# Odd token tiles on the other half of TensorE's columns, and late gate chunks beside the attention

## The chip, the cores and the metric

One Trainium2 chip, one core of it. The metric is the device time of one execution in microseconds (us), lower is better. A kernel is timed several times and the median is quoted; one more execution is taken with the hardware profiler, and every row below is from that one.

## The reference, cut to what matters

A decoder layer over 16 meta tokens and 2048 tokens of width 1024. One wide projection feeds three causal mixers with 4 heads of 128 each, a sigmoid gate weighs each mixer's projection, and the gated sum goes through `w_out`.

```
q, k, v  -> stick_breaking_attention            # o_sb, all earlier keys, blocks of 128
gq,gk,gv -> conv of width 4, silu, l2norm -> gated_delta_rule_chunked   # o_gd, unit lower triangular solves
hq,hf,hi -> hgrn2_chunked                       # o_hg, decayed scores within a chunk, a state between chunks
y   = gates[0]*(o_sb @ w_branch[0]) + gates[1]*(o_gd @ w_branch[1]) + gates[2]*(o_hg @ w_branch[2])
out = h + y @ w_out
```

## The kernel before, in words

The 2048 tokens are four **quarters** j = 0 to 3 of 512 tokens, each four **token tiles** of 128 (`NT = 4`, index n). The residual width lies on the 128 partitions in 8 pieces. Numbers are float32; a product of two such values is made of three matmuls of 128x512 (`mm3`, lines 167 to 169: high by high, high by low, low by high).

**Dense work** is the generator `dense_work`. Its unit is a **chunk**: 24 matmuls of 128x512 that project the 512 tokens on 128 columns of `w_in` (`proj`), followed by one evacuation. In a quarter there are 16 chunks for the attention (`sb_proj`: K, Q, V, gate for 4 heads), one small one (`gdn_rows`), 12 **conv chunks** for the delta rule (`gdn_proj`, `conv`), 4 gates, 16 for HGRN2, 24 **mix gate chunks** (`branch`, 8 for each mixer, evacuated by one sigmoid on ScalarE, line 1212) with 24 **products** of 12 matmuls each, and 8 output chunks (`outp`). A conv chunk gives VectorE three multiply-adds (line 730) and one product (line 734).

**Scans** are the parts with a chain of dependent steps. `sb_scan` is one head's attention: scores `z` on TensorE, two sigmoids on ScalarE (lines 522, 523), a running product on VectorE (line 528), a multiply (line 534, VectorE and GpSimd by turns), then four transposes (line 558), a copy to the high part (line 562, ScalarE), the low part (line 118, VectorE), and three matmuls into `av`. In quarter j it runs over j+1 blocks of keys. `gdn_mats` and `gdn_scan` are the delta rule: `gdn_scan` inverts 32x32 blocks on VectorE, joins them to 64x64 (lines 920 to 944) and to 128x128 (its **last step**, lines 959 and 969), then runs the recurrence over the token tiles (lines 991 to 1014). `hg_scan` is HGRN2 for one head: seven **levels** s = 1, 2, 4, ..., 64, with a matmul per token tile and block in each. Levels 1 to 16 (line 1148) use all four quarters of the output partitions, level 32 (line 1135) two of them (b and b+32 rows from b = 0 and 64), level 64 (line 1126) the lower half alone; ScalarE copies what 32 and 64 give into `at` (lines 1140 and 1130).

**The order.** The main loop weaves each scan with a counted number of dense chunks: a chunk ends with an `END`, `adv(n)` emits n of them, `weave(scan, us, n)` spreads n over a scan by the estimated times in the list `US`. In quarter j, `adv(5)` and four attention scans (4, 4, 4 and 5 chunks) come first, then `gdn_mats` (3 each), `gdn_scan` (11), and so on. The program is then built with `schedule_with_timeline_sim=True`: a scheduler reorders what was emitted, within the buffers, so that a stretch of the built program can hold more dense chunks than its `weave` counted. Each engine runs its own list in that order. A product of mixer 0 needs the attention of all four heads (`obs[0, h]`), and the gate tiles of mixers 0 and 1 have two buffers (`g`), so before the last head is done at most two or three mix gate chunks can run.

Of the kernel before, what the change touches and what calls it, by code (L numbers as in the profile page):

```python
# [39 lines left out]
def kernel(  # L40
# [830 lines left out]
    def gdn_scan(j, st):  # L871
# [82 lines left out]
        for g in range(2):  # L954
            pT = (p_z, p_tr)[g]()
            pT3 = pT.rearrange("p (h n c) -> p h n c", h=2, n=NT)
            for h in range(2):
                for n in range(NT):
                    nc.tensor.matmul(
                        pT3[64:128, h, n], u[2 * g + h][0:64, n, 64:128], x2[g][0:64, h, n], start=True, stop=True  # L960
                    )
            (nc.scalar.copy, nc.vector.tensor_copy)[g](x2[g][64:128], pT3[64:128])
        yield 2.0
        for g in range(2):
            pU = (p_z, p_tr)[g]()
            pU3 = pU.rearrange("p (h n c) -> p h n c", h=2, n=NT)
            for h in range(2):
                for n in range(NT):
                    nc.tensor.matmul(
                        pU3[0:64, h, n], x2[g][64:128, h, n], u[2 * g + h][64:128, n, 64:128], start=True, stop=True  # L970
                    )
                (nc.scalar.copy, nc.vector.tensor_copy)[g](u[2 * g + h][0:64, :, 64:128], pU3[0:64, h])
# [121 lines left out]
    def hg_scan(j, h, st):  # L1094
# [10 lines left out]
        while s < P:  # L1105
# [17 lines left out]
            if s == 64:  # L1123
                for n in range(NT):
                    c = META + n * P
                    nc.tensor.matmul(
                        z[:64, n * 64 : (n + 1) * 64], kql[:, c : c + 64], kql[:, c + 64 : c + P],
                        start=True, stop=True,
                    )
                nc.scalar.copy(at[:64, :, 64:], z[:64, :256].rearrange("p (n c) -> p n c", n=NT))  # L1130
            elif s == 32:
                for n in range(NT):
                    for b in (0, 64):
                        c = META + n * P + b
                        nc.tensor.matmul(
                            z[b : b + 32, n * 32 : (n + 1) * 32], kql[:, c : c + 32], kql[:, c + 32 : c + 64],
                            start=True, stop=True,
                        )
                for b in (0, 64):
                    nc.scalar.copy(  # L1140
                        at[b : b + 32, :, b + 32 : b + 64],
                        z[b : b + 32, :128].rearrange("p (n c) -> p n c", n=NT),
                    )
# [60 lines left out]
    def branch(j, xs, b, obs, y, yh, yl, lag=0):  # L1204

        gs, ws = {}, {}

        def gate(e):
            gs[e] = slot("D", (P, TQ)) if b == 2 else slot("g", (P, TQ))
# [5 lines left out]
        def product(e):  # L1215
# [8 lines left out]
            if b == 0:  # L1224
                y[e] = slot("y", (P, TQ))
# [77 lines left out]

    def dense_work():
# [39 lines left out]
    US = (  # L1344
        [CHUNK_US] * 29 + [B_US] * 5 + [CHUNK_US] * 4 + [B_US] * 3 + [CHUNK_US] * 8 + [B_US] * 2
        + [CHUNK_US] * 4 + [B_US] * 2 + [CHUNK_US] * 4 + [B_US] * 4 + [CHUNK_US] * 4 + [B_US] * 4
        + [3 * END] * 4 + [CHUNK_US] * 8
    )

# [15 lines left out]
    def weave(scan, scan_us, n):  # L1365

        upto = ends[0] + n
        us = sum((US + US)[ends[0] % len(US) :][:n])
# [76 lines left out]
    for j in range(nq):  # L1445
        adv(5 if j else 3)
        sb_us = 4 * (2.0 + 2.7 * j) + 0.8 * (5 + 4 * j)
        for h in range(H):
            obs[0, h] = weave(sb_scan(j, h, sst), sb_us, 4 + (h == H - 1))
        for h in range(H):  # L1450
# [4 lines left out]
        adv(5)  # L1455
        for h, o_ in enumerate(weave(both(hg_scan(j, 0, hst), hg_scan(j, 1, hst)), 2 * HG_US, 7)):
            obs[2, h] = o_
        adv(5)
# [90 lines left out]
```

## Time and profile before

| | |
|---|---|
| median of 3 runs | 2812.92 us (2812.78 to 2814.28) |
| the profiled execution, its own time | 2815.66 us |
| its span, first to last instruction | 2813.9 us |
| TensorE busy / VectorE / ScalarE / GpSimd | 98% / 52% / 34% / 26% of the span |
| mean granted TensorE clock | 0.995 of full speed |

The span is what the trace shows; 1.8 us of the profiled execution's time lie outside it. Busy time of TensorE counts overlapping matmuls once. A 128x512 matmul is shown as some 0.39 us long, but the next starts 0.23 us after it, so its cost is read from start to start. A float32 matmul that is not split by hand (lines 920 to 1185) stands in the trace as two instructions.

### The profile page before, as it was taken

The page shows a single profiled execution, that of the slowest core. Times are in us where ns is not written, and L with a number is a line of the kernel's source. Part 1 is how long each engine was busy: PE and PEld are TensorE (multiplying, and loading weights), DVE is VectorE, ACT ScalarE, POOL GpSimd, SP SyncE. Part 2 cuts the span into 40 slices and gives each one's busy share as a digit, 9 for nine tenths or more (in the row PEclk, how much of TensorE's full clock was granted, in tenths as well). Part 3 has the DMA queues.
Part 4 walks back from the last instruction along what each step waited for, and adds up shares of the span by engine and source line. Part 5 has one row for each costly group of instructions (what it writes and reads, how often), then busy time and mean ns, then how long its engine had stood idle before and what let it go on. Part 6 is the DMA issues. An engine that isn't in the chain of part 4 may idle for free.

```text
span 2813.9 us, 46012 instructions
## 1 busy us (share of the span) xinstructions
PE 2758.2 (98%) x17616; PEld 2273.7 (81%) x17616; DVE 1469.7 (52%) x2878; ACT 953.8 (34%) x2195; POOL 738.4 (26%) x1011
## 2 busy tenths in 40 slices
PE   7999999999999999999999999999999999999999
PEld 7898787888887888878887778887888777788887
DVE  5466637745357545543256754454325677527521
ACT  5454234243345212222244531221224555113120
POOL 4555214433132302112023330111212222302111
PEclk9999999999999999999999999999999999999999
DMA  7667746679554654547754356344764434653556
GB/s 256 228 202 250 256 163 218 227 256 322 188 172 149 193 170 130 152 149 249 228 177 161 129 164 187 121 150 151 246 211 145 135 119 143 196 160 125 158 157 210
DMA packets 200064, 520.51 MB, mean 185 GB/s; under 512 B 43104, under 2 KB 44064, under 8 KB 199844
## 3 DMA queue, kind: packets, MB, share of 16 engines
q1 hardware_dynamic: 199556, 517.50, 56.6%
q8 instruction: 139, 2.28, 0.3%
q14 instruction: 81, 0.66, 0.1%
q10 hardware_dynamic: 288, 0.07, 0.0%
HBM read 397.18 MB, written 120.31 MB: 184 GB/s over the span
## 4 chain that ended last, share of the span: by engine, by line
PE 90%; DVE 5%; DMA 2%; ACT 1%; issue 1%; POOL 1%; SPq 0%; DVEq 0%; POOLq 0%; ACTq 0%
PE acc L167 21%; PE acc L168 20%; PE acc L169 20%; PE av L167 4%; PE av L168 4%; PE av L169 4%; PE tr L558 2%; PE acc L380 1%; PE tr L380 1%; DVE D L730 1%; PE z L167 1%; PE z L168 1%; PE z L169 1%; PE z L1148 1%; PE z L832 1%
## 5 line engine op out<-in xcount | busy, mean ns | idle before, releaser
L167 PE MATMUL acc<-xh,w 128*128 128x512 f32 (+2 forms) x2224 | 854.2, 384 | 5.7 <-DMA w<-wk 1.8
L168 PE MATMUL acc<-xl,w 128*128 128x512 f32 (+2 forms) x2224 | 839.6, 378 | 0.3 <-DVE xl L260 0.2
L169 PE MATMUL acc<-xh,w 128*128 128x512 f32 (+2 forms) x2224 | 837.4, 377 | 1.3 <-DVE w L118 1.3
L167 PEld LDWEIGHTS acc<-xh,w 128*128 128x128 f32 x2224 | 422.5, 190 | 82.0 <-DMA w<-wk 2.6
L169 PEld LDWEIGHTS acc<-xh,w 128*128 128x128 f32 x2224 | 422.6, 190 | 74.7 <-DVE w L118 2.0
L168 PEld LDWEIGHTS acc<-xl,w 128*128 128x128 f32 x2224 | 422.3, 190 | 68.7 <-DVE xl L260 1.3
L528 DVE TENSOR_TENSOR_SCAN S<-S,zero 128x128 f32<-128x128 f32 (+4 forms) x216 | 195.9, 911 | 129.6 <-ACT S L522 114.5
L118 POOL TENSOR_TENSOR w<-wraw,w 128x512 fp32r<-128x512 f32 x106 | 148.8, 1405 | 292.1 <-ACT w L147 269.9
L534 POOL TENSOR_TENSOR S<-S,S 128x256 f32<-128x256 f32 (+2 forms) x108 | 93.8, 869 | 355.2 <-DVE S L528 234.1
L522 ACT ACTIVATE S<-z,rq 128x128 f32<-128x128 f32 (+4 forms) x216 | 117.0, 542 | 125.7 <-PE z L169 80.7
L147 ACT CAST w<-wraw 128x512 fp32r<-128x512 f32 x182 | 112.5, 619 | 134.5 <-PE acc L169 63.3
L730 DVE SCALAR_TENSOR_TENSOR D<-D,cw,D 128x512 f32<-128x512 f32 (+1 forms) x144 | 124.6, 866 | 18.2 <-ACT D L728 16.2
L167 PE MATMUL av<-xh,w 128*128 128x512 f32 (+2 forms) x328 | 128.8, 393 | 1.1 <-ACT D L1050 1.1
L167 PE MATMUL acc<-ob,w 128*128 128x512 f32 x316 | 127.1, 404 | 2.1 <-ACT ob L401 1.4
L168 PE MATMUL av<-xl,w 128*128 128x512 f32 (+2 forms) x328 | 127.6, 389 | 0.0
L169 PE MATMUL av<-xh,w 128*128 128x512 f32 (+2 forms) x328 | 127.1, 388 | 0.0
L118 DVE TENSOR_TENSOR S<-tr,S 128x512 fp32r<-128x512 f32 (+4 forms) x176 | 104.9, 605 | 41.6 <-ACT S L562 41.2
L168 PE MATMUL acc<-ob,w 128*128 128x512 f32 x316 | 126.4, 401 | 0.0
L169 PE MATMUL acc<-ob,w 128*128 128x512 f32 x316 | 124.9, 396 | 0.0
L523 ACT ACTIVATE S<-z,rq 128x128 f32<-128x128 f32 (+4 forms) x216 | 116.4, 539 | 1.0 <-POOL S L527 0.9
L562 ACT CAST S<-tr 128x512 fp32r<-128x512 f32 (+4 forms) x176 | 91.2, 530 | 63.5 <-PE tr L558 63.4
L1230 POOL TENSOR_TENSOR y<-y,g 128x512 f32<-128x512 f32 x32 | 45.2, 1416 | 256.7 <-DVE g L1228 256.7
(386 smaller groups left out, 4931.1 us busy)
## 6 DMA issues: line engine op xcount, KB each, us to landing
w<-wk SPq DMA_DIRECT2D x555, 512.0 KB, 3.5
wk<-w SPq DMA_DIRECT2D x184, 512.0 KB, 3.6
wraw<-in_w_in_dram SPq DMA_DIRECT2D x142, 256.0 KB, 3.8
D<-in_xq_dram SPq DMA_DIRECT2D x56, 256.0 KB, 4.3
S<-rows SPq DMA_DIRECT2D x48, 256.0 KB, 4.9
S<-dv SPq DMA_DIRECT2D x48, 256.0 KB, 4.3
out_dram<-D SPq DMA_DIRECT2D x32, 256.0 KB, 4.3
S<-dk SPq DMA_DIRECT2D x24, 264.0 KB, 4.5
```

The lines of the kernel that those rows point to most:

```text
L118: (eng or nc.gpsimd).tensor_sub(out_, a, hi.bitcast(F32))
L147: nc.scalar.copy(hi, raw)
L167: nc.tensor.matmul(dst, lh, rh, start=first, stop=False)
L168: nc.tensor.matmul(dst, lh, rl, start=False, stop=False)
L169: nc.tensor.matmul(dst, ll, rh, start=False, stop=last)
L380: nc.tensor.transpose(pt[:, n * P : (n + 1) * P], src[:, META + n * P : META + (n + 1) * P], ident)
L522: nc.scalar.activation(pc[:, :n], z[:, :n], AF.Sigmoid, scale=rq[:, NT + i : NT + i + 1])
L523: nc.scalar.activation(at[:, :n], z[:, :n], AF.Sigmoid, scale=rq[:, i : i + 1])
L528: nc.vector.tensor_tensor_scan(pc[:, 0:n][:, ::-1], pc[:, 0:n][:, ::-1], zero1.broadcast_to([P, n]), 1.0 if carry[i] is None else pc[:, n ...
L534: eng.tensor_mul(at[:, :n], at[:, :n], pc[:, 1 : n + 1])
L562: nc.scalar.copy(ath[:kw, cs_], tr[:kw, cs_])
L730: nc.vector.scalar_tensor_tensor(dst[:, c0:], raw[:, c0 + i : c0 + i + n], cw[:, ci, i : i + 1], dst[:, c0:], ALU.mult, ALU.add)
```

## The change

First, three groups of small matmuls send odd token tiles to another part of the output partitions. Level 64: tiles 1 and 3 write partitions 64 to 127 instead of 0 to 63. Level 32: tiles 1 and 3 write 32 rows further up, so that all four quarters are used. Last step of the inverses: tiles alternate between the halves. Each copy that follows becomes two, one for the even tiles and one for the odd tiles.

Second, in quarters 2 and 3 (`j >= AHEAD`) the branch of mixer 0 runs with a lag of 5: its first five gate chunks are emitted directly behind `sb_proj`, three gates with products follow behind `gdn_proj`, and the last five products behind the first head's HGRN2 chunks. These gates lie in the tiles `y`, of which there are eight, and the product is written over the gate. The counts of the main loop and the list `US` follow. Quarters 0 and 1 are emitted as before.

```diff
         for g in range(2):
             pT = (p_z, p_tr)[g]()
-            pT3 = pT.rearrange("p (h n c) -> p h n c", h=2, n=NT)
+            pT3 = pT[:, :256].rearrange("p (h n c) -> p h n c", h=2, n=2)
             for h in range(2):
                 for n in range(NT):
+                    o = 64 * (1 - n % 2)
                     nc.tensor.matmul(
-                        pT3[64:128, h, n], u[2 * g + h][0:64, n, 64:128], x2[g][0:64, h, n], start=True, stop=True
+                        pT3[o : o + 64, h, n // 2], u[2 * g + h][0:64, n, 64:128], x2[g][0:64, h, n],
+                        start=True, stop=True,
                     )
-            (nc.scalar.copy, nc.vector.tensor_copy)[g](x2[g][64:128], pT3[64:128])
+            for i in range(2):
+                o = 64 * (1 - i)
+                (nc.scalar.copy, nc.vector.tensor_copy)[g](x2[g][64:128, :, i::2], pT3[o : o + 64])
...
                 for n in range(NT):
+                    o = 64 * (n % 2)
                     nc.tensor.matmul(
-                        pU3[0:64, h, n], x2[g][64:128, h, n], u[2 * g + h][64:128, n, 64:128], start=True, stop=True
+                        pU3[o : o + 64, h, n // 2], x2[g][64:128, h, n], u[2 * g + h][64:128, n, 64:128],
+                        start=True, stop=True,
                     )
...
                 for n in range(NT):
-                    c = META + n * P
+                    c, o = META + n * P, 64 * (n % 2)
                     nc.tensor.matmul(
-                        z[:64, n * 64 : (n + 1) * 64], kql[:, c : c + 64], kql[:, c + 64 : c + P],
+                        z[o : o + 64, n // 2 * 64 : n // 2 * 64 + 64], kql[:, c : c + 64], kql[:, c + 64 : c + P],
...
                     for b in (0, 64):
-                        c = META + n * P + b
+                        c, o = META + n * P + b, b + 32 * (n % 2)
                         nc.tensor.matmul(
-                            z[b : b + 32, n * 32 : (n + 1) * 32], kql[:, c : c + 32], kql[:, c + 32 : c + 64],
-                            start=True, stop=True,
+                            z[o : o + 32, n // 2 * 32 : n // 2 * 32 + 32], kql[:, c : c + 32],
+                            kql[:, c + 32 : c + 64], start=True, stop=True,
                         )
...
+        tag = "D" if b == 2 else ("y" if lag else "g")
+
         def gate(e):
-            gs[e] = slot("D", (P, TQ)) if b == 2 else slot("g", (P, TQ))
+            gs[e] = slot(tag, (P, TQ))
...
             if b == 0:
-                y[e] = slot("y", (P, TQ))
+                y[e] = g if lag else slot("y", (P, TQ))
...
+            ahead = 5 * (j >= AHEAD)
+            b0 = branch(j, xs, 0, obs, y, yh, yl, ahead)
+            yield from take(b0, ahead)
             yield from gdn_rows(j, xs, gst)
             yield from gdn_proj(j, xs, range(H), gst)
             pool_share[0] = 2
-            b0 = branch(j, xs, 0, obs, y, yh, yl)
-            yield from take(b0, 5)
+            yield from take(b0, 3 if ahead else 5)
             yield from gdn_gates(j, xs, range(H), gst)
-            yield from take(b0, 3)
+            if not ahead:
+                yield from take(b0, 3)
             yield from hg_proj(j, xs, 0, hst)
+            if ahead:
+                yield from take(b0, 5)
...
+        adv(5 * (j >= AHEAD))
         for h in range(H):
             weave(gdn_mats(j, h, gst), 8.0, 3)
```

**ScalarE, head 1's attention in the last quarter, its second half.** The names are those of the tiles: `S` scores and weights, `z` and `tr` of the attention, `acc` a dense chunk's result. Before, its evacuations of chunks there are those of `gdn_rows` (L628) and of the first conv chunk (L725):

```order
L562 CAST S_22274<-tr_22269 128x512
L522 ACTIVATE S_22285<-z_22281,rq_21243 128x272
L523 ACTIVATE S_22286<-z_22281,rq_21243 128x272
L522 ACTIVATE S_22302<-z_22298,rq_21243 128x272
L523 ACTIVATE S_22303<-z_22298,rq_21243 128x272
L628 COPY D_22862<-acc_22865 100x512
L725 COPY D_22998<-acc_23004 128x512
```

In the changed kernel the first chunks in that head's scan are mix gates (L1228, into `y`):

```order
L1228 ACTIVATE y_22908<-acc_22913 128x512
L522 ACTIVATE S_22074<-z_22070,rq_21289 128x512
L523 ACTIVATE S_22075<-z_22070,rq_21289 128x512
L562 CAST S_22095<-tr_22090 128x512
L522 ACTIVATE S_22106<-z_22102,rq_21289 128x512
L523 ACTIVATE S_22107<-z_22102,rq_21289 128x512
L562 CAST S_22124<-tr_22119 128x512
L1228 ACTIVATE y_23051<-acc_23056 128x512
L1228 ACTIVATE y_23157<-acc_23162 128x512
```

Five gate chunks have moved ahead of `gdn_rows` and the conv chunks; those follow later in the same attention.

**VectorE, head 2's attention in quarter 2, ahead of the first line 118 of that head.** `S` are attention tiles, `D` those of conv chunks (L730, L734), `tr` the transposed weights. (A running product of line 528 is listed here as a SCALAR_TENSOR_TENSOR.) Before, conv work stands in the row:

```order
L701 SCALAR_TENSOR_TENSOR D_16288<-D_16288,zero_380 16x128
L730 SCALAR_TENSOR_TENSOR D_16087<-D_16088,cw,D_16087 128x512
L704 MEMSET D_16288 16x1
L734 TENSOR_TENSOR D_16087<-D_16087,D_16088 128x512
L528 SCALAR_TENSOR_TENSOR S_15637<-S_15637,zero_380 128x512
L534 TENSOR_TENSOR S_15638<-S_15638,S_15637 128x512
L730 SCALAR_TENSOR_TENSOR D_16211<-D_16212,cw,D_16211 128x512
L367 TENSOR_REDUCE nv_16191<-acc_16425 128x4
L118 TENSOR_TENSOR S_15668<-tr_15662,S_15667 128x512
```

In the changed kernel the row is attention work alone:

```order
L528 SCALAR_TENSOR_TENSOR S_15592<-S_15592,zero_380 128x128
L534 TENSOR_TENSOR S_15593<-S_15593,S_15592 128x128
L528 SCALAR_TENSOR_TENSOR S_15615<-S_15615,zero_380 128x256
L528 SCALAR_TENSOR_TENSOR S_15633<-S_15633,zero_380 128x384
L534 TENSOR_TENSOR S_15634<-S_15634,S_15633 128x384
L528 SCALAR_TENSOR_TENSOR S_15648<-S_15648,zero_380 128x512
L528 SCALAR_TENSOR_TENSOR S_15673<-S_15673,zero_380 128x512
L534 TENSOR_TENSOR S_15674<-S_15674,S_15673 128x512
L118 TENSOR_TENSOR S_15704<-tr_15698,S_15703 128x512
```

The conv chunks' multiply-adds have moved behind it, into the later part of the attention.

**TensorE, the last step of the inverses in the last quarter.** `z` and `tr` are the results of two pairs of heads, `acc` is dense work. Before, dense matmuls stand between line 959 and line 969 (20 of them, four shown):

```order
L959 MATMUL z_24903<-S_24737,S_23749 64x64 x4
L959 MATMUL z_24903<-S_24737,S_23947 64x64 x4
L959 MATMUL tr_24913<-S_24738,S_24165 64x64 x4
L959 MATMUL tr_24913<-S_24738,S_24373 64x64 x4
L169 MATMUL acc_25327<-xh_20649,w_5017_25323 128x512
L167 MATMUL acc_25327<-xh_20687,w_5017_25323 128x512
L168 MATMUL acc_25327<-xl_20688,w_5017_25323 128x512
L169 MATMUL acc_25327<-xh_20687,w_5017_25323 128x512
```

In the changed kernel the same step (lines 960 and 974 there) and the recurrence (from line 1000) follow one another:

```order
L960 MATMUL z_25016<-S_24868,S_23950 64x64 x4
L960 MATMUL z_25016<-S_24868,S_24148 64x64 x4
L960 MATMUL tr_25027<-S_24869,S_24366 64x64 x4
L960 MATMUL tr_25027<-S_24869,S_24565 64x64 x4
L974 MATMUL z_25044<-S_23950,S_24868 64x64 x4
L974 MATMUL tr_25057<-S_24366,S_24869 64x64
L1000 MATMUL z_25083<-Sg_404,S_23920 128x128
L974 MATMUL tr_25057<-S_24366,S_24869 64x64 x3
L1000 MATMUL tr_25085<-Sg_405,S_24118 128x128
```

No dense matmul stands between these steps, nor in the rest of that recurrence. In quarter 2 dense matmuls remain between them.

## Rows read from the trace of the kernel before

**Rows 1.** The page: busy time, share of the span and instructions of each engine.

```profile
PE 2758.2 (98%) x17616; PEld 2273.7 (81%) x17616; DVE 1469.7 (52%) x2878; ACT 953.8 (34%) x2195; POOL 738.4 (26%) x1011
```

**Rows 2.** Windows, attention of quarters 2 and 3: length, busy us per engine, clock, DMA.

```profile
1518.00:1587.00 69.00, 66.33 (x344) 53.64 (x343) 53.08 (x80) 38.10 (x80) 22.96 (x45) 1.00 0.44 142
1587.00:1656.00 69.00, 63.92 (x313) 51.10 (x312) 44.88 (x71) 34.70 (x75) 20.47 (x34) 0.95 0.37 122
2073.00:2180.00 107.00, 106.59 (x540) 87.09 (x539) 48.16 (x72) 42.50 (x84) 23.23 (x42) 1.00 0.48 158
2180.00:2245.00 65.00, 62.26 (x322) 49.18 (x321) 40.86 (x65) 38.42 (x79) 18.42 (x35) 1.00 0.42 131
2245.00:2325.00 80.00, 74.21 (x369) 59.45 (x368) 62.28 (x89) 43.82 (x89) 22.98 (x43) 0.96 0.38 124
2325.00:2402.00 77.00, 72.33 (x368) 57.94 (x367) 55.60 (x84) 41.96 (x86) 21.60 (x35) 1.00 0.44 144
```

**Rows 3.** TensorE's waits from 2200 to 2410 us: total, times, longest.

```profile
PE av L168 <- DVE S L118: 5.1, 8, 1.6
PE tr L558 <- POOL S L534: 1.7, 1, 1.7
PE acc L167 <- ACT ob L401: 1.4, 1, 1.4
```

**Rows 4.** TensorE's waits from 1500 to 1665 us.

```profile
PE av L168 <- DVE S L118: 2.8, 2, 1.6
PE acc L167 <- DMA w<-wk: 1.6, 1, 1.6
```

**Rows 5.** Timeline of TensorE, two heads' levels 32 and 64: start, length, count.

```profile
1850.15 0.45 PE L1135 MATMUL z<-S 128*32 128x32 f32 x16
1850.52 1.15 PE L1126 MATMUL z<-S 128*64 128x64 f32 x16
1851.60 0.50 PE L169 MATMUL av<-xh,w 128*128 128x512 f32 x1
```

**Rows 6.** Timeline of TensorE, part of a level that uses four partition quarters.

```profile
1826.58 0.33 PE L1148 MATMUL z<-S 128*32 128x32 f32 x16
```

**Rows 7.** Timeline of TensorE, last step of the inverses in quarter 0.

```profile
352.83 1.14 PE L959 MATMUL z<-S,S 64*64 64x64 f32 x16
353.81 1.09 PE L959 MATMUL tr<-S,S 64*64 64x64 f32 x16
354.84 0.50 PE L169 MATMUL av<-xh,w 128*128 128x512 f32 x1
...
359.58 0.68 PE L969 MATMUL z<-S,S 64*64 64x64 f32 x8
360.10 0.63 PE L969 MATMUL tr<-S,S 64*64 64x64 f32 x8
```

**Rows 8.** Groups on ScalarE, shapes apart: the copies that are cut in two.

```profile
L1140 ACT COPY AT<-z 32x128 f32<-32x128 f32 x32 | 8.2, 256 | 10.5 <-PE z L1135 10.2
L1130 ACT COPY AT<-z 64x256 f32<-64x256 f32 x16 | 5.9, 367 | 18.2 <-PE z L1126 17.8
L962 ACT COPY S<-z 64x512 f32<-64x512 f32 x4 | 2.3, 581 | 8.2 <-PE z L959 8.2
```

**Rows 9.** Timeline: ScalarE's copies of level 64, and TensorE's first reader of them.

```profile
1851.24 0.83 ACT L1130 COPY AT<-z 64x256 f32<-64x256 f32 x2
...
1860.92 0.39 PE L1183 MATMUL tr<-D,AT 128*128 128x128 f32 x2
```

**Rows 10.** Groups on VectorE, shapes apart: a conv chunk's work.

```profile
L730 DVE SCALAR_TENSOR_TENSOR D<-D,cw,D 128x512 f32<-128x512 f32 x108 | 89.8, 832 | 15.8 <-ACT D L728 14.5
L734 DVE TENSOR_TENSOR D<-D,D 128x512 f32<-128x512 f32 x36 | 26.3, 730 | 12.0 <-ACT D L733 12.0
```

**Rows 11.** Timeline of TensorE in the last quarter, first matmul of two recurrence steps.

```profile
2535.89 0.39 PE L991 MATMUL z<-Sg,S 128*128 128x128 f32 x2
...
2540.66 0.39 PE L991 MATMUL z<-Sg,S 128*128 128x128 f32 x2
```

More of the change, by code (lines that the diff above doesn't have):

```diff
@@ L965, in gdn_scan @@
             pU = (p_z, p_tr)[g]()
-            pU3 = pU.rearrange("p (h n c) -> p h n c", h=2, n=NT)
+            pU3 = pU[:, :256].rearrange("p (h n c) -> p h n c", h=2, n=2)
             for h in range(2):
                 for n in range(NT):
+                    o = 64 * (n % 2)
                     nc.tensor.matmul(
-                        pU3[0:64, h, n], x2[g][64:128, h, n], u[2 * g + h][64:128, n, 64:128], start=True, stop=True
-                    )
-                (nc.scalar.copy, nc.vector.tensor_copy)[g](u[2 * g + h][0:64, :, 64:128], pU3[0:64, h])
+                        pU3[o : o + 64, h, n // 2], x2[g][64:128, h, n], u[2 * g + h][64:128, n, 64:128],
+                        start=True, stop=True,
+                    )
+                for i in range(2):
+                    (nc.scalar.copy, nc.vector.tensor_copy)[g](
+                        u[2 * g + h][0:64, i::2, 64:128], pU3[64 * i : 64 * i + 64, h]
+                    )
         if m0:
@@ L1124, in hg_scan @@
                 for n in range(NT):
-                    c = META + n * P
+                    c, o = META + n * P, 64 * (n % 2)
                     nc.tensor.matmul(
-                        z[:64, n * 64 : (n + 1) * 64], kql[:, c : c + 64], kql[:, c + 64 : c + P],
+                        z[o : o + 64, n // 2 * 64 : n // 2 * 64 + 64], kql[:, c : c + 64], kql[:, c + 64 : c + P],
                         start=True, stop=True,
                     )
-                nc.scalar.copy(at[:64, :, 64:], z[:64, :256].rearrange("p (n c) -> p n c", n=NT))
+                for g in range(2):
+                    nc.scalar.copy(
+                        at[:64, g::2, 64:], z[64 * g : 64 * g + 64, :P].rearrange("p (n c) -> p n c", n=2)
+                    )
             elif s == 32:
@@ L1133, in hg_scan @@
                     for b in (0, 64):
-                        c = META + n * P + b
+                        c, o = META + n * P + b, b + 32 * (n % 2)
                         nc.tensor.matmul(
-                            z[b : b + 32, n * 32 : (n + 1) * 32], kql[:, c : c + 32], kql[:, c + 32 : c + 64],
-                            start=True, stop=True,
+                            z[o : o + 32, n // 2 * 32 : n // 2 * 32 + 32], kql[:, c : c + 32],
+                            kql[:, c + 32 : c + 64], start=True, stop=True,
                         )
                 for b in (0, 64):
[L1140 to L1143, printed above, removed]
+                    for g in range(2):
+                        nc.scalar.copy(
+                            at[b : b + 32, g::2, b + 32 : b + 64],
+                            z[b + 32 * g : b + 32 * g + 32, :64].rearrange("p (n c) -> p n c", n=2),
+                        )
             else:
@@ L1302 @@
     sst, gst, hst = {}, {}, {}
+    AHEAD = 2
     def dense_work():
@@ L1367, in weave @@
         upto = ends[0] + n
-        us = sum((US + US)[ends[0] % len(US) :][:n])
+        us = sum(US[ends[0] :][:n])
         due = 0.0
```

14 lines of the change are left out of this document (9 added, 5 removed).

## The prediction, made before the changed kernel had run

> **What bounds the kernel now.** I read four views in this order. The page's first part says that TensorE is busy for 2758.2 of 2813.9 us [rows 1], so time is won in two ways only: less time of TensorE, or fewer of its 55.7 idle us. The windows say where the second kind lies. In quarters 2 and 3, with several blocks of earlier keys, five stretches of the attention lose 2.67, 5.08, 2.74, 5.79 and 4.67 us (length less busy), 20.95 us in sum [rows 2]. The stretch of 107 us ahead of the third one loses 0.41. The reader is to see VectorE beside it: 45% busy in the calm stretch, 63 to 78% in the five. Two of the five also show a granted clock of 0.95 and 0.96, that is some microseconds at 1.2 instead of 2.4 GHz; 0.05 x 69 and 0.04 x 80 make 3.45 and 3.2 us lost. So 27.6 us is all that a better cover of the attention could give back. The waits name the late engine: in both quarters most of the time goes to line 118 on VectorE, the low part of the attention weights [rows 3, 4]. Then there are a multiply on GpSimd (1.7), the last head's output for the first product (1.4), and a weight load at the end of quarter 2's attention (1.6).
>
> The timelines show the first kind, the small matmuls. They stand in the middle of dense work that starts as soon as they end, so each nanosecond of them is on the path.
>
> **The change part by part: odd tiles on other columns.** What a matmul costs is read from start to start.
> - Last step of the inverses: 32 instructions of line 959 take from 352.83 to 354.84, 2.01 us; the first 16 take 0.98, 61 ns each, and 8 of line 969 take 0.52 [rows 7]. 16 in 0.98 and 8 in 0.52 mean 57 ns for one and 0.06 for the entry.
> - Level 64: two heads' 16 instructions take 1.08 us until dense work goes on, 67 ns each with entry and exit; all write the same half [rows 5].
> - Level 32: 16 instructions in two quarters of the partitions take 0.37, 23 ns each [rows 5].
> - What stands for the result is line 1148, which goes round all four quarters: 16 instructions show as 0.33 us, against 0.45 for the 16 of level 32 [rows 5, 6]. Both lengths end with the last matmul's own, so 0.12 us is the gain of four quarters over two. Two quarters against one is the same step for 64 columns: I take it that a pair costs what one cost, half of 57 to 61, 30 ns saved for each instruction.
>
> The counts: 64 instructions of lines 959 and 969 in a quarter, 256 in all, and 8 of level 64 for each of 16 heads' scans, 128. 384 x 30 ns = 11.5 us. Level 32 has 16 scans at 0.12 us, 1.9 us. The sum is 13.4; I take 13. Entry and exit stay. The bounds: nothing, if the halves take turns, and 13.4 above. Below nothing: if each change of half cost an entry, 0.06 us for each of the 192 written matmuls with 64 columns (two instructions each) makes +11.5, and for each instruction +23. Line 1148 lies nearest, and it speaks for the whole saving.
>
> The Trainium skill, page "TensorEngine Tiling (Array Packing)", section "Instruction Overhead", says that a matmul has an overhead of some 60 cycles, that one column takes as long as 60, and that no tiling should be taken from a dimension that is already small; 60 cycles at 2.4 GHz are 25 ns by estimate. By that, level 32 with its 32 columns would gain nothing and the sum would be 11.5. The trace disagrees already: 16 in 0.37 us are below that floor.
>
> The copies: a 64x256 copy takes 367 ns and a 64x512 one 581, so 0.84 ns for each column and some 150 ns fixed; each cut costs ScalarE those 150 ns once more [rows 8]. 16 + 32 + 4 + 8 cuts make 9 us on an engine that is busy 34%. They lie behind other work: the level 64 copies of two heads end at 1852.07, and the first matmul that reads them starts at 1860.92, 8.9 us later [rows 9]. If that cover were gone, one head's chain would end 0.45 us later (three of its cuts).
>
> **The change part by part: gates beside the attention.** No work is added; 5 gate chunks of 24 x 0.23 = 5.5 us each change places in two quarters. A conv chunk asks VectorE for 3 x 0.832 + 0.730 = 3.2 us [rows 10], a gate chunk for nothing (one sigmoid on ScalarE). In the built order of quarter 2, before, four conv chunks stand ahead of head 2's first `av` matmul, and their work stands ahead of line 118 on VectorE; now none does (the VectorE rows of the change), and the twelve spread to the end of head 3. So head 2's stretch should fall to the calm rate: 2.67 to 0.3, 2.4 us won. Behind the attention dense work now stands ahead of the first product, which covers the weight load: 1.6 us. With fewer waits ahead of it I take the half clock of that quarter as gone: 3.4 us. In quarter 3 the gates fill head 1's stretch (the ScalarE rows of the change): 2.74 to 0.25, 2.5 us. But the conv chunks then stand against heads 2 and 3 nearly as before, four ahead of head 2's first `av` matmul and one or two ahead of head 3's. So I give these two stretches nothing: 5.79, 4.67 and 3.2 us stay.
>
> What is late next: quarter 3's delta rule, where the dense filler has been used up (the TensorE rows of the change). The recurrence itself hardly needs it: before, a step of 40 instructions with no dense work in between already ran from 2535.89 to 2540.66, 0.12 us each [rows 11]. The joint between lines 959 and 969 does: two copies of a half, 2 x 0.367 us [rows 8], and their hand-over stand against about 0.5 us of matmuls of the other pair. I put 2 us on the waits there and at the next joint (bounds 0 and 5, the five joints of the chain at 1 us each). SP's queue gets the same weight loads in another order; the DMA share in these stretches is 0.37 to 0.48, against 0.48 in the calm one [rows 2], so I cost it at nothing, and at one wait of 1.6 us a quarter if that fails [rows 4].
>
> Sum of this part: -2.4 - 1.6 - 3.4 - 2.5 + 2 = -7.9. With the small matmuls -13 - 8 = -21 us. The profiled execution took 2815.66 us (span 2813.9 and 1.8 around it) and would take 2794.7; the median of the runs lies 2.7 lower, at 2812.92, and so goes to **2792**.
>
> **The rivals.**
> - All stalls go. For it: one late multiply-add on VectorE can start a row of waits. Against it: quarter 3's conv chunks. 13 + 27.6 gives 2772; with part of it left, up to 2785.
> - The stalls only move: the conv chunks stand against later heads, the clock falls elsewhere, and the delta rule waits 5 us. Then only the small matmuls count: 2800, between 2797 and 2806.
> - The halves take turns, so that the columns bring nothing: -8, 2805. Against it: level 32 and line 1148 differ by 0.12 us [rows 5, 6].
> - A floor for each small matmul, whichever columns it uses: level 32 stays at its 23 ns, 1.9 us are lost, 2794. Against it: line 1148 [rows 6]. It is what the rule of the Trainium skill quoted above would do here.
> - Slower: each change of half costs an entry as the one from dense work does. 192 to 384 entries of 0.06 us make +11.5 to +23, less 8 of the gates: 2816 to 2828. It decides from about 35 ns for each of the 384 instructions with 64 columns. Against it: line 1148 changes its quarter in nearly every instruction and shows no such cost [rows 6].
>
> **How the numbers follow.** Chances: as worked out (2786 to 2799) 0.55; stalls only move 0.20; all stalls go 0.12; slower 0.06; halves take turns 0.04; the floor 0.03. The range that leaves out 2 in 10 runs from 2780 (most stalls gone) to 2805 (gates bring nothing and the columns part of their gain). A measurement of this kernel tells some 0.2%, 5.6 us, from no change. Faster by more than that: all but the slower rival and the upper ends of two others, 0.87; within it 0.07; slower 0.06.
>
> **What would show it.** Level 64's 8 instructions and lines 959 and 969 at about half their start to start time; level 32 near line 1148. TensorE's busy time lower by about 13 us less what waits hide. Windows of quarter 2's heads 2 and 3 with under 4 us idle together and full clock; quarter 3's head 1 under 0.5, its heads 2 and 3 as before. Waits of a few us at lines 960 to 1000 of quarter 3. It is wrong if the small matmuls keep 57 ns, or if the sum of idle time in quarters 2 and 3 does not fall.

## The result, and the profile after

The changed kernel took 2780.41 us (median of 4 runs, 2779.08 to 2782.89) against 2812.85 us before (4 runs, 2807.57 to 2814.28). The ratio is 0.9883, 95% interval 0.9868 to 0.9897: 32.4 us faster, with 29.0 to 37.1 in the interval. The forecast was 21 us and 2792. The direction is right, and the measured time stands at the lower end of the range (2780); the size was a third short.

The page of the changed kernel, its busy times, beside [rows 1]:

```profile
PE 2734.3 (98%) x17616; PEld 2258.6 (81%) x17616; DVE 1469.8 (53%) x2890; ACT 962.5 (35%) x2255; POOL 744.0 (27%) x1011
```

TensorE issues as many matmuls as before and is busy 23.9 us less. ScalarE has 60 copies more and 8.7 us more work (forecast 9), and nothing waited for it because of them. The span is 2779.8, so 45.5 us are idle instead of 55.7. Not all of the 34.1 us between the two profiled executions is the change. Quarter 0, where only the small matmuls differ, ended 9.4 us earlier, but in the trace of before TensorE stood at half clock there for 13.6 us, which costs up to 6.8, and in the trace of the changed kernel for none (last section).

Windows of the changed kernel: quarter 2's heads 2 and 3 and the delta rule's matrices behind them, quarter 3's heads 1, 2 and 3, then the matrices and the recurrence in quarter 3. They answer to [rows 2].

```profile
1504.00:1568.00 64.00, 63.67 (x326) 51.70 (x325) 39.04 (x66) 35.39 (x73) 14.66 (x35) 1.00 0.47 151
1568.00:1633.00 65.00, 64.55 (x339) 52.64 (x337) 49.64 (x76) 37.23 (x77) 23.70 (x41) 1.00 0.44 147
1633.00:1717.00 84.00, 84.00 (x415) 69.86 (x413) 55.61 (x114) 17.17 (x42) 27.05 (x43) 1.00 0.67 207
2153.50:2237.50 84.00, 83.97 (x425) 68.41 (x425) 41.87 (x65) 40.09 (x80) 18.03 (x34) 1.00 0.46 151
2237.50:2318.50 81.00, 77.18 (x386) 62.45 (x386) 60.28 (x88) 44.84 (x91) 26.66 (x44) 0.96 0.42 133
2318.50:2397.50 79.00, 76.10 (x381) 61.47 (x380) 55.65 (x82) 41.71 (x86) 23.42 (x35) 0.98 0.47 148
2397.50:2477.00 79.50, 78.49 (x387) 64.99 (x389) 48.16 (x100) 10.45 (x26) 23.07 (x39) 1.00 0.67 206
2477.00:2525.00 48.00, 47.34 (x482) 40.98 (x481) 26.20 (x91) 18.56 (x70) 6.11 (x7) 0.96 0.26 79
```

Length less TensorE's busy time is what a stretch is said to lose, here and below: 0.33, 0.45, 0.03, 3.82 and 2.90 us in the heads, where it was 2.67, 5.08, 2.74, 5.79 and 4.67. The wait for the last head's output (1.4) stands at the border between head 3's window and that of the matrices, so quarter 3's head 3 is best taken together with the matrices: 3.9 now, 5.0 before. VectorE has moved with it: 39 of 64 us in quarter 2's head 2, 53 of 69 before. The three longest waits of the changed kernel in quarter 3's attention, beside [rows 3]:

```profile
PE av L168 <- DVE S L118: 3.1, 5, 1.5
PE acc L167 <- ACT ob L401: 1.4, 1, 1.4
PE tr L558 <- POOL S L534: 1.4, 1, 1.4
```

The same engine is late as before, at fewer places. TensorE's timeline shows the small matmuls, beside [rows 5, 7]: lines 960 and 974 are the inverses' last step, 1148 is level 32, 1136 level 64.

```profile
347.59 0.68 PE L960 MATMUL z<-S,S 64*64 64x64 f32 x16
348.11 0.63 PE L960 MATMUL tr<-S,S 64*64 64x64 f32 x16
348.67 0.50 PE L169 MATMUL av<-xh,w 128*128 128x512 f32 x1
...
352.82 0.45 PE L974 MATMUL z<-S,S 64*64 64x64 f32 x8
353.10 0.40 PE L974 MATMUL tr<-S,S 64*64 64x64 f32 x8
...
1823.44 0.33 PE L1148 MATMUL z<-S 128*32 128x32 f32 x16
1823.70 0.45 PE L1136 MATMUL z<-S 128*64 128x64 f32 x8
1824.08 0.49 PE L167 MATMUL av<-xh,w 128*128 128x512 f32 x1
```

From start to start, 32 instructions of the last step take 1.08 us instead of 2.01, 8 of line 974 take 0.28 instead of 0.52, and level 32's sixteen 0.26 instead of 0.37.

### The profile page after: what moved, and what is told of

Same layout as the page of the kernel before. It is cut to its first block, busy times and chain, and to the rows that moved or that the text cites. A ratio compares the mean times of both kernels' runs of the same rounds, so it can differ in the third digit from the quotient of the medians.

```text
span 2779.8 us, 46064 instructions
## 1 busy us (share of the span) xinstructions
PE 2734.3 (98%) x17616; PEld 2258.6 (81%) x17616; DVE 1469.8 (53%) x2890; ACT 962.5 (35%) x2255; POOL 744.0 (27%) x1011
## 5 line engine op out<-in xcount | busy, mean ns | idle before, releaser
L730 DVE SCALAR_TENSOR_TENSOR D<-D,cw,D 128x512 f32<-128x512 f32 (+1 forms) x144 | 120.2, 835 | 17.2 <-ACT D L728 15.0
L167 PE MATMUL av<-xh,w 128*128 128x512 f32 (+2 forms) x304 | 119.7, 394 | 0.7 <-ACT D L1059 0.7
L168 PE MATMUL av<-xl,w 128*128 128x512 f32 (+2 forms) x304 | 118.1, 389 | 0.0
L169 PE MATMUL av<-xh,w 128*128 128x512 f32 (+2 forms) x304 | 117.5, 386 | 0.0
```

What stands on the lines that cost most here:

```text
L167: nc.tensor.matmul(dst, lh, rh, start=first, stop=False)
L168: nc.tensor.matmul(dst, lh, rl, start=False, stop=False)
L169: nc.tensor.matmul(dst, ll, rh, start=False, stop=last)
L730: nc.vector.scalar_tensor_tensor(dst[:, c0:], raw[:, c0 + i : c0 + i + n], cw[:, ci, i : i + 1], dst[:, c0:], ALU.mult, ALU.add)
```

## The experiments

Each run is given against runs of the kernel before on the same chip. The table sets the quarters side by side: the time from the last output addition of the quarter before to that of this one, in the profiled execution, against the kernel before (664.55, 705.41 and 742.73 us). Executions of one order differ by some microseconds: quarter 3 in the order of the changed kernel shows -7.7 to -12.1 in four of them (rows 1, 6, 11 and 12).

```
                                   median   before    ratio (95%)              Q1     Q2     Q3
changed kernel                     2780.41  2812.85   0.9883 (.9868-.9897)   -4.1  -12.9   -7.7
columns alone                      2799.42  2814.07   0.9947 (.9935-.9960)   -3.7   -4.4   -3.9
gates alone                        2796.22  2814.07   0.9936 (.9922-.9949)   -0.1  -11.3   -7.2
gates behind the conv chunks       2798.25  2814.07   0.9945 (.9933-.9958)   -4.1   -5.6   -3.0
conv with less VectorE work        2797.62  2813.40   0.9946 (.9933-.9960)   -0.1   -8.9   -6.6
tile order 0, 2, 1, 3              2780.50  2813.40   0.9885 (.9870-.9899)   -3.3  -14.2   -9.4
eight gates ahead                  2789.77  2813.40   0.9918 (.9904-.9931)   -4.0  -13.4   -2.2
turns in quarter 3                 2778.05  2813.40   0.9875 (.9862-.9889)   -3.5  -14.4  -14.2
three gates, then turns            2781.33  2815.25   0.9880 (.9865-.9895)   -4.1  -12.9  -10.2
eight gates, more beside matrices  2798.05  2815.25   0.9940 (.9928-.9953)   -4.0   -8.9   -1.7
gates ahead in quarter 3 only      2789.43  2814.86   0.9907 (.9892-.9922)   -4.1   -4.5  -12.1
gates ahead from quarter 1         2785.39  2814.86   0.9891 (.9875-.9908)   +2.5  -14.4   -9.5
```

**The kernel before, once more.**

> The kernel before, once more. In its first trace quarter 0 shows the granted clock at 0.98 from 150 to 430 us (three stretches at half clock, near 170, 221 and 337 us, 13.6 us in sum, so 6.8 us lost at the most), and the trace of the changed kernel shows full clock there, although code and order are the same in both until about 345 us. Theory A, chance: a second execution of the same kernel has its half clock stretches elsewhere, and not these three. Theory B, it belongs to the kernel: the same three stretches come again, at the same instructions. The span is 2811 to 2814 us by both.

It took 2812.23 us (one run; the span of 2810.5 is just under the 2811 to 2814 expected). Its window from 150 to 345 us has the clock at 0.98, where the first trace of before has 0.96; the stretch from 340 to 430 is at 1.00 now (0.98 then). The half clock comes at 170 and 221 us again, as in the first trace; only the stretch at 337 us is missing, and none has come elsewhere in the quarter. So theory A, other places, did not hold, and theory B holds for two of the three: the place belongs to the kernel, and whether the clock falls there belongs to the execution (last section).

It also answers another question, how much a wait costs that the windows show as little idle time. TensorE's timeline in quarter 3's head 1 (start, length, in brackets the idle time and its releaser):

```profile
2213.16 0.48 PE L167 MATMUL av<-S,S 128*128 128x512 f32 x1
2213.84 0.51 PE L168 MATMUL av<-S,S 128*128 128x512 f32 x1 [0.20 <-DVE S L118]
2214.18 0.40 PE L169 MATMUL av<-S,S 128*128 128x512 f32 x1
2214.80 0.50 PE L167 MATMUL av<-S,S 128*128 128x512 f32 x1 [0.22 <-ACT S L562]
2215.71 0.50 PE L168 MATMUL av<-S,S 128*128 128x512 f32 x1 [0.41 <-DVE S L118]
2216.05 0.39 PE L169 MATMUL av<-S,S 128*128 128x512 f32 x1
```

Undisturbed matmuls of this size start 0.23 us apart and are drawn 0.39 long. Here three starts follow after 0.68, 0.62 and 0.91: 0.45, 0.39 and 0.68 us lost, where the view shows 0.20, 0.22 and 0.41 idle. Each of these three waits hides 0.17 to 0.27 us under the drawn length of the matmul before it.

**The columns alone.** The last step and levels 32 and 64 as in the change, the gates and all counts as before.

> Only the small matmuls' columns; the gates stay where they were. The prediction: -13 us. Read from the trace after (quarter 1, whose order did not change, is 3.9 us shorter): -15.5 us, with 2.5 us more than the start to start times of the instructions themselves give. If the rest of the result comes from the clock of quarter 0 and the columns bring that too: -21 us. Level 64's eight instructions and lines 959 and 969 at about half of 57 ns by all of them.

-14.65 us, with -18.3 to -11.3 in the interval: 13 and 15.5 both lie in it, 21 doesn't. The start to start times within these groups of instructions, summed over the whole trace, fall from 32.1 to 19.2 us. The windows of the attention are as before (TensorE 65.70 of 68.40 us in quarter 2's head 2), so this part touches no stall.

**The gates alone.** All of the change but the columns.

> Only the gate chunks beside the attention; the small matmuls are as before. The prediction: -8 us. Stalls only move: 0 to -5 us. Read from the trace after (quarter 2 gives 9.5 and quarter 3 gives 3.8 us beyond what quarter 1 gives): -13 us, with quarter 3's heads 2 and 3 losing about 7 us together instead of 10.5. If the two parts don't touch each other, this run and the run of the columns alone sum to the -32.4 us of both; if they do, the sum is off by more than 3 us.

-17.85 us, -21.9 to -14.4 in the interval: more than any of the three said. With the columns' -14.65 it makes -32.5, and both together made -32.4. Each of these is known to some 4 us, and within that the two parts don't touch each other. Its page and its windows, quarter 2's heads 2 and 3 and quarter 3's heads 1 to 3:

```profile
PE 2747.8 (98%) x17616; PEld 2271.1 (81%) x17616; DVE 1467.3 (53%) x2878; ACT 954.8 (34%) x2195; POOL 740.8 (27%) x1011
```

```profile
1516.70:1580.50 63.80, 63.52 (x324) 51.47 (x324) 39.06 (x66) 35.16 (x72) 14.19 (x35) 1.00 0.48 151
1580.50:1645.60 65.10, 64.65 (x339) 52.73 (x338) 49.76 (x75) 37.41 (x77) 23.16 (x41) 1.00 0.45 146
...
2167.50:2251.50 84.00, 83.92 (x426) 68.35 (x425) 41.88 (x64) 40.05 (x80) 18.09 (x34) 1.00 0.46 151
2251.50:2332.50 81.00, 77.21 (x387) 62.50 (x387) 60.38 (x88) 44.99 (x92) 26.57 (x44) 0.96 0.42 134
2332.50:2410.10 77.60, 74.56 (x381) 59.92 (x379) 55.00 (x81) 42.09 (x86) 21.50 (x35) 1.00 0.48 150
```

TensorE's waits from 1500 to 1656 us, beside [rows 4], are these two alone:

```profile
PE acc L176 <- POOL nr L125: 0.4, 1, 0.4
PE acc L694 <- DVE D L683: 0.3, 1, 0.3
```

Of the 19.5 us between this profiled execution and that of before (span 2794.4 against 2813.9), 9.1 are idle time and 10.4 are busy time, though the matmuls are the same: half of the gain doesn't show as idle time.

**The gates behind the conv chunks.**

```diff
-            yield from take(b0, ahead)
             yield from gdn_rows(j, xs, gst)
             yield from gdn_proj(j, xs, range(H), gst)
+            yield from take(b0, ahead)
```

> The changed kernel, but in quarters 2 and 3 the five gate chunks are issued behind the conv chunks instead of ahead of them; as many chunks as in the changed kernel stand beside the attention. If the stalls went because the conv chunks with their 3.2 us of VectorE each moved away from heads 2 and 3 (the prediction's ground): the stretches of quarter 2's heads 2 and 3 lose 5 to 8 us together again, quarter 3's head 1 loses 2 to 3, and the time is 2787 to 2791. If they went because there is more dense work ahead of the first product and in the joints: 2780 to 2783, within 0.1% of the changed kernel.

2798.25, worse than either theory said. It is within noise the time of the columns alone (2799.42 on the same chip), so the gates win nothing there. The five windows:

```profile
1509.50:1577.80 68.30, 65.60 (x340) 53.17 (x339) 52.41 (x79) 37.48 (x77) 23.00 (x45) 1.00 0.44 140
1577.80:1648.70 70.90, 67.43 (x336) 54.22 (x335) 45.02 (x71) 35.37 (x76) 19.95 (x33) 0.98 0.41 134
2166.00:2232.70 66.70, 63.59 (x324) 50.48 (x323) 41.10 (x64) 38.36 (x79) 18.04 (x35) 0.97 0.40 128
2232.70:2313.10 80.40, 74.30 (x368) 59.61 (x367) 62.04 (x89) 44.07 (x89) 23.13 (x43) 0.96 0.37 122
2313.10:2401.00 87.90, 85.51 (x429) 69.28 (x428) 55.21 (x81) 43.64 (x89) 21.71 (x35) 1.00 0.47 156
```

2.70, 3.47, 3.11, 6.10 and 2.39 us idle: the stalls of before are back, with VectorE at 52 of 68 us in the first. Filler at the end of the attention is not what counted; what stands beside heads 1 to 3 is.

**Conv chunks with less work for VectorE.** The kernel before; in quarters 2 and 3 two of a convolution's three multiply-adds are left out.

```diff
-        for i in range(1, 4):
+        for i in range(1, 4 if j < 2 else 2):
```

> The kernel before, with two of the three multiply-adds of each convolution left out in quarters 2 and 3 (so its output differs); nothing is moved, and TensorE has the same work in the same order. VectorE gets 24 x 2 x 0.83 = 40 us less. If the stalls beside the attention come from the conv chunks' load on VectorE: quarter 2's heads 2 and 3 (2.67 and 5.08 us idle) and quarter 3's heads 2 and 3 (5.79 and 4.67) fall below 1 us each, but quarter 3's head 1 (2.74), where no conv chunk ends yet, stays above 2; the time falls by 15 to 20 us. If what lacks is dense work ahead of the first product, whatever VectorE has to do: 0 to -5 us, and all five windows as before.

-15.8 us, inside the first theory's figure and far from the second's. The windows are quarter 2's heads 2 and 3 and the matrices behind them, then quarter 3's heads 1 to 3.

```profile
1515.20:1578.90 63.70, 63.70 (x338) 52.56 (x338) 43.00 (x65) 39.23 (x81) 24.06 (x45) 1.00 0.43 141
1578.90:1641.10 62.20, 61.97 (x318) 50.18 (x316) 39.04 (x61) 33.20 (x71) 17.92 (x33) 1.00 0.41 136
1641.10:1729.40 88.30, 85.98 (x406) 70.76 (x405) 47.14 (x99) 11.05 (x27) 22.65 (x40) 0.98 0.70 215
...
2168.30:2233.50 65.20, 62.49 (x324) 49.19 (x323) 40.94 (x64) 38.12 (x79) 18.41 (x35) 1.00 0.40 131
2233.50:2308.10 74.60, 71.75 (x373) 57.96 (x372) 49.88 (x74) 43.41 (x87) 21.21 (x43) 1.00 0.44 147
2308.10:2382.30 74.20, 70.94 (x367) 57.35 (x365) 47.88 (x71) 42.15 (x87) 20.52 (x35) 1.00 0.39 127
```

The stalls inside quarter 2's heads go without any move (0.00 and 0.23), and head 1 of quarter 3 keeps its 2.71, as expected. What stands behind quarter 2's head 3 stays: 2.32 us are idle in the stretch of the matrices, 1.4 for the last head's output and 0.9 for a weight load (1.97 us before). So there the second theory has a part: that stretch lost nothing in the changed kernel, where dense work stands ahead of the first product. Heads 2 and 3 of quarter 3 keep 2.85 and 3.26, where under 1 was expected: only part of their stalls is the conv chunks' load.

**Another order of the tiles.** In the small matmuls `for n in range(NT)` becomes `for n in (0, 2, 1, 3)`.

> The changed kernel with the token tiles of level 32, level 64 and the inverses' last step taken in the order 0, 2, 1, 3 instead of 0, 1, 2, 3; the columns of each tile stay. If a matmul runs beside the one before it only when the two stand on different columns: half of the 384 changes from one to the next fall back from about 30 to 57 ns, +5.2 us, and the inverses' 16 instructions show some 0.9 us from start to start where the changed kernel's take 0.63 in all. If only the number of columns in use counts and not which stands next to which: 0 us.

2780.50: no change. The 32 instructions take 1.13 us to the next dense matmul (353.68 to 354.81), against 1.08. In the changed kernel's trace starts come in pairs, 7 ns and then 51 ns apart. I read this as two rows of starts, one for each half, with 58 ns from start to start within a row. In this run the second start follows after 13 ns, and then two such rows interleave again, each at 58 ns but for one gap. If the built order is the written one, tile 1 thus started beside tile 0 although tile 2, on tile 0's half, stood between them. So the first theory, by which half of the changes fall back to 57 ns, did not hold: the tiles need not alternate one by one. All of one half's tiles ahead of the other's was not tried.

**All eight gates ahead.**

```diff
-            ahead = 5 * (j >= AHEAD)
+            ahead = 8 * (j >= AHEAD)
...
-            yield from take(b0, 3 if ahead else 5)
+            if not ahead:
+                yield from take(b0, 5)
...
-                yield from take(b0, 5)
+                yield from take(b0, 8)
...
-        adv(5 * (j >= AHEAD))
+        adv(8 * (j >= AHEAD))
```

> The changed kernel with all eight gates of the first branch, not five, ahead of the conv chunks in quarters 2 and 3, and its eight products behind the first head's projections of the third branch. If the conv chunks beside heads 2 and 3 are what costs: quarter 3's heads 2 and 3 (3.82 and 2.90 us idle, and two stretches at half clock) lose some 3 to 6 us less, as three conv chunks move past them, and up to 3 come back as waits at the delta rule's joints: -1 to -5 us against the changed kernel, 2775 to 2779. If the stalls only follow the conv chunks: 0, within 2 us of the changed kernel. If the delta rule then lacks filler: +2 to +5.

+9 us on the changed kernel, more than any theory. Quarter 3's heads 2 and 3, the delta rule's matrices and its recurrence, and TensorE's two longest waits in the last two of these:

```profile
2241.40:2325.50 84.10, 84.10 (x432) 68.50 (x431) 61.82 (x95) 49.74 (x99) 21.30 (x42) 1.00 0.49 158
2325.50:2409.90 84.40, 84.40 (x433) 69.16 (x433) 57.61 (x85) 42.55 (x89) 23.20 (x37) 1.00 0.47 146
2409.90:2487.00 77.10, 68.36 (x326) 56.80 (x324) 44.71 (x92) 8.21 (x23) 19.63 (x33) 0.96 0.63 186
2487.00:2540.00 53.00, 48.82 (x474) 43.69 (x475) 28.79 (x96) 18.84 (x71) 7.55 (x14) 0.84 0.21 65
```

```profile
PE z L832 <- DVE S L818: 6.5, 2, 3.6
PE z L941 <- DVE S L926: 2.4, 1, 2.4
```

The attention loses nothing any more, though VectorE is hardly less busy in head 2 (61.8 of 84 us, 62.3 of 80 before): so its load alone doesn't make the stalls. The place of the conv chunks in it may, or that more dense work stands beside that head (432 matmuls, 369 before); this run doesn't part the two. The delta rule pays: 8.74 and 4.18 us idle, and the clock at 0.96 and 0.84.

**Turns in quarter 3.** Gate and conv chunks by turns, there alone (`turns` takes one chunk from each generator in a round).

```diff
-            yield from take(b0, ahead)
+            gates = take(b0, ahead)
+            if j < nq - 1:
+                yield from gates
             yield from gdn_rows(j, xs, gst)
-            yield from gdn_proj(j, xs, range(H), gst)
+            yield from turns(gates, gdn_proj(j, xs, range(H), gst))
```

> The changed kernel, but in quarter 3 alone gate and conv chunks take turns (gate, conv, gate, conv, ..., then the other seven convs), so that VectorE's work is spread from head 1 to head 3. If a conv chunk costs more the closer the next one stands: quarter 3's heads 1 to 3 lose less together than the 6.75 us idle of the changed kernel, -2 to -4 us. If each conv chunk beside the attention has its price wherever it stands: head 1 stalls for 1 to 3 us again and heads 2 and 3 win as much, 0 us. If the gates are worth it only as one block ahead: +2 to +6, as the run with the gates behind the convs lost 18 in two quarters.

2778.05, the lowest median, but its interval covers the changed kernel's. Heads 1, 2, 3 of quarter 3 lose 2.93, 0.17 and 1.69: 4.8 instead of 6.75 us, at full clock. Head 1 stalls again, as the second theory says; heads 2 and 3 win more than it loses, as the first says.

**Three gates, then turns.** As before, with `take(gates, 3)` ahead in quarter 3.

> The changed kernel, but in quarter 3 three gate chunks stand ahead and the last two take turns with the first conv chunks (gate, gate, gate, conv, gate, conv, gate, conv, ...). In the changed kernel quarter 3's heads 1, 2, 3 lose 0.03, 3.82 and 2.90 us; with all five in turns they lost 2.93, 0.17 and 1.69. If head 1 needs filler (gates with no work for VectorE) and heads 2 and 3 need the conv chunks apart, and three gates are enough for head 1: under 2 us for the three together, and 2773 to 2777. If what counts is only when the first conv chunk comes (the later, the calmer heads 2 and 3): between the two, 2777 to 2780. If the two wishes exclude each other, so that a gate kept for head 1 is a stall in head 2: no better than the turns, 2778 or more.

2781.33: the third case, no better than the turns. Head 1 is calm with three gates (0.11 us idle), but heads 2 and 3 lose 2.40 and 3.39, and head 3 has the clock at 0.96.

**Eight gates, and more beside the matrices.** As the run with eight; `weave(gdn_mats(...))` takes four chunks instead of three for three heads, and the next `adv(4)` becomes `adv(1)`.

> All eight gates ahead, as in the run with eight, whose attention in quarter 3 lost nothing (84.1 of 84.1 and 84.4 of 84.4 us busy) and whose delta rule lost 8.7 and 4.2 us idle; here three more dense chunks stand beside the building of the delta rule's matrices in quarters 2 and 3, taken from the stretch of dense work alone behind the recurrence. If the delta rule lost for want of filler: the loss in quarter 3 between the attention and the end of the recurrence (12.9 us idle, and the clock) falls under 5, and the time to 2772 to 2779, below the changed kernel. If it waits for VectorE's own work (line 832 behind line 818), whatever stands beside: 2787 to 2791 as with eight.

2798.05, worse than with eight alone. In quarter 3 the matrices lose 10.3 and the recurrence 3.4 us. TensorE was busy for 67.0 us in the stretch of the matrices (68.4 with eight): the three chunks were not there. What kept them from it stays open. In quarter 2 they were there, with 560 matmuls beside the matrices instead of 488; that stretch lost 0.31 us instead of 0.77, but the recurrence behind it then lost 1.96 instead of 0.50, at a clock of 0.94, and the quarter took 4.5 us longer than with eight alone. The stretch of the matrices in quarter 2:

```profile
1636.40:1751.10 114.70, 114.39 (x560) 94.66 (x561) 66.56 (x133) 23.87 (x56) 28.23 (x50) 1.00 0.66 200
```

**Which quarter.** `AHEAD = 3`, then `AHEAD = 1`.

> The changed kernel with the gates ahead in quarter 3 only; quarter 2 goes back to the old order. By the prediction's terms quarter 2 is worth 2.4 + 1.6 + 3.4 = 7.4 us and quarter 3 only 2.5 - 2 = 0.5: +7.4 on the changed kernel, 2788. By the traces of before and of the run with the gates alone (taken between the ends of the quarters) quarter 2 is worth 11.5 and quarter 3 some 7: +11.5, 2792. If the prediction was short in quarter 3 alone: +7.4 here too, and the rest in quarter 3.

> The changed kernel with the gates ahead in quarter 1 too. There heads 1 to 3 of the attention lose 0.0, 0.4 and 0.0 us idle, before and after the change. If gate chunks ahead pay only where the attention waits: 0, within 2 us of the changed kernel, with up to 2 us lost at quarter 1's delta rule. If moving them wins something of its own (more dense work ahead of the first product, fewer waits behind): -3 us or more.

In quarter 3 only: 25.4 us under before. Quarter 2's part is thus 7.0 by the medians (32.4 less 25.4) and 9.4 by the table (-13.8, the mean of the five traces with that order and the columns and five gates, less the columns' 4.4); quarter 3's is 10.8 by the medians (25.4 less 14.65) and 7.2 by the run of the gates alone. The intervals of +-4 us don't tell 7.4 from 11.5 for quarter 2, but quarter 3's is far from 0.5.

From quarter 1 on: 29.5 under before, 3 less than the change, which lies within the intervals. The trace says more: quarter 1 takes 2.5 us longer than before, where it is 3.3 to 4.1 us shorter in the nine other traces with the columns. Its recurrence and the first pair of heads behind it:

```profile
1029.90:1105.50 75.60, 72.44 (x598) 60.35 (x598) 31.25 (x93) 19.99 (x72) 8.09 (x11) 1.00 0.37 118
1105.50:1173.70 68.20, 66.21 (x667) 53.89 (x666) 42.13 (x103) 15.67 (x50) 13.85 (x12) 1.00 0.43 134
```

3.16 and 1.99 us idle, and none in either before. In this quarter, where the attention doesn't wait, filler taken from the delta rule is only lost there.

## Why the prediction fell short

**The small matmuls: right.** -13 was forecast, -14.65 measured. By the start to start times the terms are 7.4 for the inverses' last step (forecast 256 x 30 ns = 7.7), 3.6 for level 64 (3.8) and 1.8 for level 32 (1.9), 12.8 in sum. The rivals on this part fell: the halves don't take turns, changes of half cost nothing, and level 32 did gain. Its sixteen instructions now take 0.26 us, 16 ns each instead of 23 (33 instead of 47 for each matmul, which is two of them); on one and the same quarter of the partitions I read some 32 ns from start to start, before and after, so what changed is how many quarters run side by side. The rule from the Trainium skill, page "TensorEngine Tiling (Array Packing)", section "Instruction Overhead", gives each matmul an overhead of some 60 cycles, 25 ns by estimate. That level 32 would gain nothing by it is refuted here; whether it holds as a floor for one quarter of the columns no run here shows, and the prediction's "the trace disagrees already" claimed more than its 23 ns, of two quarters side by side, could show.

**The gates: right mechanism, sum too small.** -8 was forecast, -17.85 measured. Term by term, with the windows of the gates alone:
- Quarter 2's head 2, 2.67 to 0.3: it is 0.28. Its clock back at 1.00: it is.
- Quarter 2's head 3: the prediction took 1.6 of 5.08 and let 3.5 stay. With the matrices behind it 5.5 became 0.45, 5.0 won. This is 3.4 us of the shortfall.
- Quarter 3's head 1: 2.74 to 0.25, it is 0.08.
- Quarter 3's heads 2 and 3, "nothing": head 2's 5.79 became 3.79, head 3 with the matrices 5.0 became 4.5. That is 2.5 more. The run with the gates behind says that the order of the chunks did it, the run with less conv work that VectorE's load is part of it; what the rest of these stalls hangs on stays open. The 3.2 us of half clock there stayed, as forecast.
- The delta rule's joints, +2: the recurrences of quarters 2 and 3 lose 0.72 and 1.15, where they lost 0.08 each, +1.7.

So idle time falls by 12.6 us in the attention, not by 6.5; 9.1 is left of it over the whole span, as the joints and waits behind take some back. The rest of the gain, 10.4 us, is busy time. 3.4 of it is quarter 2's half clock, which the prediction did count. The second failed step is what it did not: it measured a stall as length less busy, and what a wait hides under a drawn matmul counts as busy. TensorE's waits in quarter 2's stretch of [rows 4] and in quarter 3's attention were 8 and 22 before and are 2 and 12 with the gates alone. 16 fewer at 0.17 to 0.27 us, as in the three waits of the kernel before, are some 3.6 by estimate (2.7 to 4.3), and with the 3.4 of the clock 7; 0.8 is quarter 0, and 2.6 us are not accounted for.

**The step that failed** is therefore the sizing of the second part: "I give these two stretches nothing" and the rest of quarter 2's head 3 that was let stay (5.9 us of idle time between them), and under both the size of a stall, which was taken from idle time (by estimate some 4 us of hidden waits were left out). The rival "all stalls go" came nearest with its 2772 to 2785, though quarter 3's heads still lose 6.75 us idle. "The stalls only move" was wrong for this order and right for two neighbours of it: with the gates behind the conv chunks nothing is won, and with eight ahead the stalls stand in the delta rule.

## What to carry to other kernels

Measure a stall from start to start of the matmuls, not as window less busy time: short waits hide part of themselves under the drawn length of the matmul before, and half clock is busy time. When chunks of dense work are dealt out as filler, ask what each asks of the engine that is late there: moving five chunks that ask VectorE for nothing ahead of twelve that ask it for 3 us each was worth 18 us in this kernel, and the same five behind the twelve nothing. And filler is a fixed stock: with five chunks taken from the delta rule the sum was a gain, with eight 9 us of it were lost again, and in a quarter whose attention didn't wait five were a plain loss.

## What the runs showed of the hardware that was not expected

By the records of the single instructions, small matmuls on different halves start 7 ns apart, and 58 ns after the one before on their own half. So two halves double the rate, 29 ns for each instruction instead of 58, and strict alternation isn't needed: in the order 0, 2, 1, 3 the second row of starts began 13 ns after the first.

In quarter 0 the granted clock falls to half in 13 of the 14 traces, in code that no version changes but for the small matmuls at its end. It always falls at one or more of the same three places, near 170, 220 and 338 us, around waits of TensorE of 2.6, 2.2 and 1.2 to 1.8 us. These waits stand in all 14 traces, also in that of the changed kernel, whose clock stays at full speed there; so the waits alone don't decide it, and what does stays open. The window from 150 to 345 us, in the second execution of the kernel before and then in the changed kernel:

```profile
150.00:345.00 195.00, 186.19 (x1322) 165.93 (x1321) 132.74 (x236) 87.24 (x192) 92.51 (x115) 0.98 0.72 235
```

```profile
150.00:345.00 195.00, 184.66 (x1325) 164.05 (x1324) 134.62 (x238) 88.38 (x196) 92.83 (x115) 1.00 0.73 240
```

The first execution of before shows 0.96: 13.6 us at half clock, up to 6.8 us lost. This is more than some of the effects studied here. It is why single traces are compared by quarter, and why the medians decide.
